# A hybrid encoder layer on one core: a parked residual gets its norm's g and b on return, attention chains start apart, merged rows are transposed per group

## The chip, the cores and the metric

The kernel runs on one core of a Trainium2 chip. The metric is device time in microseconds (us) of one execution. The five engines of the core work through their own queues in order: PE (TensorE: matmuls and transposes), DVE (VectorE), ACT (ScalarE), POOL (GpSimd) and SP (SyncE, which here only issues DMAs). A line such as L1164 is a line of the kernel before.

## What is computed

One layer over 256 rows of 2048 channels, all in float32, in this order:

```python
x = layer_norm(ALPHA * x + 0.5 * swiglu(x, ffn1), ln1_g, ln1_b)
mix = hybrid_mixer(x, w_in, ..., w_up_m, w_up_sb, w_out)
x = layer_norm(ALPHA * x + mix, ln2_g, ln2_b)
x = layer_norm(ALPHA * x + 0.5 * swiglu(x, ffn2), ln3_g, ln3_b)
x = x + sigmoid(x @ w_ple_gate) * (p @ w_ple_proj)
```

The mixer multiplies x by `w_in` and cuts the result into the inputs of two attention branches and two gates. One branch is an mLSTM with 4 heads of 256 channels; the other is stick-breaking attention with 8 heads of 128 channels. Then `merged = sigmoid(ga) * (y_m @ w_up_m) + sigmoid(gb) * (y_sb @ w_up_sb)`, and `mix = merged @ w_out`. The first norm's result x is needed twice: at once as the mixer's input, and at the end of the mixer as the residual `ALPHA * x`.

## The kernel before

**Matmuls.** Each weight tile has 256 rows and up to 512 columns and comes by one 512 KB DMA on SP's queue (L1133) into a page of a pool of 44 pages. It is split into a high part (a cast on ACT, L1160) and a low part (a subtraction on DVE, L1164). The left operand is split in the same way, and each product is three matmuls, high by high, high by low and low by high (L1211 to L1213). A unit is one weight tile against 128 rows: two blocks of 128 weight rows, so six matmuls. There are 1560 units, most weight tiles have two (one for each half of the rows, t = 0 and 1). The two gates of the mixer, as the FFN's two up projections, go through a seven-product scheme (`seven`, L321), whose sums of weights are made on DVE (L342) or by accumulating DMAs on POOL's queue (L337).

**Order of the work.** The order of instructions is written out by a planner in the program itself. `program` is a list of units; a unit adds 6 x 0.2161 us for 512 columns (half for 256) to a planned clock, `sched.now` (L1214). Everything else (norms, attention, transposes) is a generator that yields planned delays; after each unit, `sched.run()` emits the steps that have come due, and then `splits_due()` emits splits until the stage's number of weight tiles lies split ahead. `rooms(a, b)` sets these limits for the mixer: a tiles loaded, b tiles split. So a step's due time decides only its place in each engine's queue; in the run, each engine goes on as soon as what it needs is there. A step that is due between two units is emitted after the next unit.

**The first norm.** `Norm.load` (L403) loads g and b twice: as columns (L413, L414), and as rows broadcast to 128 partitions (L409, L410: four pages of 128x1024). `finish` normalizes the residual `xres` in place without g and b (L442); `turn` transposes it on PE and applies g and b there as per-partition scale and bias, which is the mixer's input. When the last `turn` is done, `rows` (L471) is spawned with a delay of 30.0: eight steps 6.0 apart, each of two DVE instructions over 128x512 (L478 times g, L479 plus b), bring `xres` itself to its final value. Then `spill` (L605) parks `xres` in DRAM by two POOL DMAs, because its room serves the merged gates of the mixer (`gt`, L949). `refill` (L612) brings it back by eight SP DMAs (L616) before `out_done` (L1018) adds the mixer's result.

**Stick-breaking attention.** `stick(h)` (L873) is a chain for one head: scores on PE (L878), four ACT instructions (copy, abs, exp, ln), a DVE and a POOL step, cumulative sums on PE (L891), a DVE step, exp on ACT (L895), a POOL step, the product with v on PE (L902), and four pairs of ACT and DVE splits. Two sequences run beside the weight stream, heads 0, 2, 4, 6 and heads 1, 3, 5, 7 (L936). Each chain waits for flags: `sb_turn` (L671) transposes q and k and sets its flag as soon as its DVE copy (L680) is emitted; v's flag is set at L665. The chains' columns of `w_in` come in the order of L930: k and v of heads 4 to 7 and then q of heads 6 and 7 (256 columns) come last.

**The merge.** Columns are merged in four groups of 512. `ups(g, 0)` and `ups(g, 1)` multiply by the two up weights; `up_done` (L982) applies the gates on DVE (L986) and adds (L989). `merge_turn` (L994) transposes a merged block for `w_out` (`transposed`, L264). The blocks of groups 0 to 2 are transposed together, after the third group (L1011); the refill follows 14.0 after that point (L1012); group 3's are transposed as they come. In this stage six weight tiles lie split ahead (L1008).

Of the kernel before, what the change touches and what calls it, by code (L numbers as in the profile page):

```python
# [13 lines left out]
P = 128  # L14
S = 256
TT = S // P
D = 2048
# [25 lines left out]

DELAY = {
    "gb": 12.0, "form": 14.0, "form1": 30.0, "ln_turn": 3.4, "ln_step": 1.2, "ln_low": 2.6, "h": 8.0, "silu": 6.0, "late": 9.0, "rest": 1.2, "mt": 3.2,
    "sbt": 6.0, "g0": 3.0, "g1": 4.0, "g2": 12.0, "cv0": 1.0, "cv1": 6.0, "turn": 3.5, "away": 6.0, "cv2": 1.3,
    "m0": 3.0, "m1": 0.6, "m2": 1.2, "m3": 4.6, "m4": 4.6, "s0": 6.6, "s1": 6.7, "s2": 4.0,
}

# [131 lines left out]
def kernel(  # L181
# [26 lines left out]
    def temp():  # L208
        sched.until(lambda: temps[0] < TEMP_BUFS)
        temps[0] += 1  # L210
        return temp_pool.tile([P, COL], F32, name="temp", tag="temp")

    def drop(n=1):
        temps[0] -= n
# [4 lines left out]
    def big(shape=(P, 1024)):  # L219
        return page_pool.tile(list(shape), F32, name="big", tag="page")  # L220
# [11 lines left out]
    def use_table(func):  # L232
        if func in tables and tables[func] != table[0]:
            table[0] = tables[func]
            nc.scalar.preload_act_table_set(table[0])  # L235
# [154 lines left out]
    def rooms(*n):  # L390
        return lambda: room.__setitem__(slice(0, len(n)), n)
# [5 lines left out]
    class Norm:  # L397
# [4 lines left out]

        def load(self):  # L403
            use_table(ACT.Sqrt)
            self.g, self.b = [big(), big()], [big(), big()]
            pages[0] += 4
            for k in range(2):
                ks = slice(k * 1024, (k + 1) * 1024)
                nc.sync.dma_start(out=self.g[k][:], in_=self.g_in[ks].partition_broadcast(P))  # L409
                nc.sync.dma_start(out=self.b[k][:], in_=self.b_in[ks].partition_broadcast(P))  # L410
            raw = temp()
            n = D // P
            nc.sync.dma_start(out=raw[0:n, 0:P], in_=self.g_in.rearrange("(c q) -> c q", q=P))  # L413
            nc.sync.dma_start(out=raw[n:2 * n, 0:P], in_=self.b_in.rearrange("(c q) -> c q", q=P))  # L414
            sched.spawn(self.columns(raw, n), DELAY["gb"])

        def columns(self, raw, n):
            ps = misc([P, 2 * n])
# [29 lines left out]
        def turn(self, t, c):  # L448
            act = self.act
            ps = misc([P, 4, P])  # L450
            for k in range(4):
                nc.tensor.transpose(ps[:, k], xres[t][:, (4 * c + k) * P:(4 * c + k + 1) * P], ident[:])  # L452
            y = whole(act, c, t) if act.forms else temp()[:]
            for k in range(4):
                g, b = (self.gb[:, i, 4 * c + k:4 * c + k + 1] for i in range(2))
                activate(y[:, k * P:(k + 1) * P], ps[:, k], ACT.Identity, scale=g, bias=b)
            dst, y = act.get(c, t), y.rearrange("q (k s) -> q k s", s=P)
            nc.scalar.copy(dst[:, 0], y)
            yield DELAY["ln_low"]
            nc.vector.tensor_tensor(out=dst[:, 1], in0=y, in1=dst[:, 0], op=ALU.subtract)  # L460
            if not act.forms:
                drop()
            finished(act, c, t)
            self.left -= 1
            if self.left == 4 and held[0] == 1:
                held[0] = 2
            if self.left == 0:
                held[0] = 0
                sched.spawn(self.rows(), self.delay)

        def rows(self):  # L471
            for c in range(4):
                for t in range(TT):
                    xs = xres[t][:, c * COL:(c + 1) * COL]
                    gs = slice((c % 2) * COL, (c % 2 + 1) * COL)
                    g, b = self.g[c // 2][:, gs], self.b[c // 2][:, gs]
                    if self.alpha is None:
                        nc.vector.tensor_tensor(out=xs, in0=xs, in1=g, op=ALU.mult)  # L478
                        nc.vector.tensor_tensor(out=xs, in0=xs, in1=b, op=ALU.add)  # L479
                    else:  # L480
                        nc.vector.scalar_tensor_tensor(out=xs, in0=xs, scalar=self.alpha, in1=g,
                                                       op0=ALU.mult, op1=ALU.mult)
                        nc.vector.scalar_tensor_tensor(out=xs, in0=b, scalar=self.alpha, in1=xs,
                                                       op0=ALU.mult, op1=ALU.add)
                    yield self.step
            pages[0] -= 4
            if self.then:
                self.then()


    def scaled(xs):
# [102 lines left out]
        yield  # L594

    x1T = ActT(act_tile, ActT(act_tile), "form1")
    norm1 = Norm(ln1_g[0], ln1_b[0], x1T, None, 30.0, 6.0, lambda: sched.spawn(spill(), 6.0))
    ffn(ffn1_w1[0], ffn1_w3[0], ffn1_w2[0], xT, norm1, skew=False, ahead=[lambda: mixer_setup()])


# [4 lines left out]
    def spill():  # L605
        for t in range(TT):
            nc.gpsimd.dma_start(out=kept[t][:], in_=xres[t][:])
        flags.add("spilt")
        return
        yield  # L610

    def refill():  # L612
        for c in range(4):
            for t in range(TT):
                cs = slice(c * COL, (c + 1) * COL)
                nc.sync.dma_start(out=xres[t][:, cs], in_=kept[t][:, cs])  # L616
        flags.add("refilled")
        return
        yield


    def mixer_setup():
# [22 lines left out]
    def wait(*names):  # L645
        while not all(f in flags for f in names):
            yield 0.6
# [23 lines left out]
    def sb_turn(name, t, stage, h0, n):  # L671
        ps = misc([P, 4, P])
        for k in range(n):
            nc.tensor.transpose(ps[:, k], stage[:, k * P:(k + 1) * P], ident[:])
        a = h0
        while a < h0 + n:
            b = min(h0 + n, (a // 4 + 1) * 4)
            if (name, "T", a // 4) not in st:
                st[name, "T", a // 4] = big().rearrange("q (h s) -> q h s", s=S)
            nc.vector.tensor_copy(out=st[name, "T", a // 4][:, a % 4:a % 4 + b - a, t * P:(t + 1) * P],  # L680
                                  in_=ps[:, a - h0:b - h0])
            a = b
        drop()
        flags.update((name, t, h) for h in range(h0, h0 + n))
        return
        yield


    stage_g = {}
# [182 lines left out]

    def stick(h):  # L873
        yield from wait(*[(n, t, h) for n in ("sq", "sk", "sv") for t in range(TT)])
        q, k = st["sq", "T", h // 4][:, h % 4], st["sk", "T", h // 4][:, h % 4]
        ps = misc([P, 3 * P])
        for s in range(2):
# [40 lines left out]
    head = group(w_in, range(0, D, 2 * P), 0, COL, x1T, qk_done(0, 0))  # L918
    program.extend(skewed(head[:SKEW]) + flat(head[SKEW:]))
    program.extend(columns(4096, 2 * HM + 2 * DS, gates_done))  # L920
    main = [rooms(10, 4)] + columns(1024, COL, qk_done(1, 0)) + [rooms(8)]
    for g in range(2):
        if g:
            main += [rooms(9)] + columns(COL, COL, qk_done(0, 1)) + [rooms(9)] + columns(1024 + COL, COL, qk_done(1, 1))
# [5 lines left out]
    for first, n in ((2, 4), (8, 4), (16, 4), (12, 4), (20, 4), (6, 2)):  # L930
        main += columns(sq0 + first * DS, n * DS, lambda ps, t, f=first, n=n: sb_columns(ps, t, f, n))
        if first in (2, 20):
            main.append(rooms(12 if first == 2 else 10))
        if first == 16:
            main.append(rooms(11))
            main.append(lambda: [sched.spawn(in_sequence([stick(a), stick(a + 2), stick(a + 4), stick(a + 6)]))  # L936
                                 for a in (0, 1)])

# [43 lines left out]
    def up_done(g, half):  # L982
        def done(ps, t):
            sched.until(lambda: ("gate", g, half, t) in flags)
            a = gt[g, t][:, half * COL:(half + 1) * COL]
            nc.vector.tensor_tensor(out=a, in0=ps, in1=a, op=ALU.mult)  # L986
            if half:
                m = gt[g, t][:, 0:COL]
                nc.vector.tensor_tensor(out=m, in0=m, in1=a, op=ALU.add)  # L989
                if g == 3:  # L990
                    sched.spawn(merge_turn(g, t), DELAY["mt"])
        return done

    def merge_turn(g, t):  # L994
# [13 lines left out]
    program.append(rooms(10, 6))  # L1008
    for g in range(3):
        program.extend(ups(g, 1))  # L1010
    program.append(lambda: [sched.spawn(merge_turn(g, t), 1.0 + 2.0 * g + t) for g in range(3) for t in range(TT)])  # L1011
    program.append(lambda: sched.spawn(refill(), 14.0))  # L1012
    program.extend(ups(3, 0) + ups(3, 1))

    x2T = ActT(act_tile, ActT(act_tile))
# [2 lines left out]
    def out_done(g):  # L1018
        def done(ps, t):
            xs = xres[t][:, g * COL:(g + 1) * COL]  # L1020
            assert "refilled" in flags
            nc.vector.scalar_tensor_tensor(out=xs, in0=xs, scalar=ALPHA, in1=ps, op0=ALU.mult, op1=ALU.add)
            norm2.chunk(t, g)
        return done
# [226 lines left out]
```

## Time and profile before

| | |
|---|---|
| median of 3 runs | 2209.06 us (2208.79 to 2209.24) |
| the profiled execution | 2208.55 us, of which the profile's span is 2206.8 us |
| busy: PE / DVE / ACT / POOL | 2182.0 / 1789.7 / 1334.4 / 233.0 us |
| mean granted clock of TensorE | 0.997 |
| DMA | 527.06 MB, 239 GB/s in the mean |

An engine's busy time is the time in which the profile shows an instruction of it. PE's ends are modelled, so its busy time hides small losses; they are better read from the waits, from the granted clock (PEclk, as a share of full speed) and from the starts of single matmuls. In a row of the timeline, the first number is the start in us from the start of the span, the second is how long the row's instructions took together, and the bracket at the end tells how long the engine stood idle before it and what ended that.

### The profile page before, as it was taken

The numbers are of one execution on the slowest core, as the hardware profiler recorded it, in microseconds if no ns is written. First come the engines' busy times: TensorE is split into PE (matmuls) and PEld (weight loads), VectorE is DVE, ScalarE is ACT, GpSimd is POOL, SyncE is SP. The second block draws the span as 40 slices with busy tenths as digits, with TensorE's granted clock in tenths as the row PEclk, the third lists the DMA queues.
The fourth block names the chain that finished last, engine by engine and source line by source line (L and its number), as shares of the span: only waits on it lengthen the run. The fifth ranks groups of instructions, "written<-read, shape, count | busy, mean of one in ns | idle before, by whom it ended". The sixth has DMA issues, their size and how long they took to land.

```text
span 2206.8 us, 27786 instructions
## 1 busy us (share of the span) xinstructions
PE 2182.0 (99%) x9972; PEld 1805.6 (82%) x9972; DVE 1789.7 (81%) x1967; ACT 1334.4 (60%) x1600; POOL 233.0 (11%) x209
## 2 busy tenths in 40 slices
PE   9999999999999999999999999999999999999999
PEld 7888888888887878888887888888888888888878
DVE  6889988888898878877675876599898989889884
ACT  6556556666575556766565634556665666666562
POOL 3111001110100011011021000011011101110000
PEclk9999999999999999999999999999999999999999
DMA  9899889987992778879777875579879998989652
GB/s 347 221 254 269 257 241 298 270 246 215 281 352 80 229 192 253 230 224 269 214 191 220 268 235 185 206 172 316 251 236 248 303 257 250 247 269 300 218 166 73
DMA packets 274346, 527.06 MB, mean 239 GB/s; under 512 B 16640, under 2 KB 25760, under 8 KB 273952
## 3 DMA queue, kind: packets, MB, share of 16 engines
q1 hardware_dynamic: 229248, 435.10, 58.2%
q0 software_dynamic: 44960, 90.19, 22.2%
q8 instruction: 78, 1.28, 0.2%
q14 instruction: 60, 0.49, 0.1%
HBM read 518.93 MB, written 6.29 MB: 238 GB/s over the span
## 4 chain that ended last, share of the span: by engine, by line
PE 93%; DVE 2%; ACT 2%; DMA 1%; issue 1%; DVEq 0%; ACTq 0%
PE mm L1212 25%; PE mm L1213 25%; PE mm L1211 25%; PE seeded L1212 5%; PE seeded L1213 5%; PE seeded L1211 5%; DMA raw<-in_ffn_w_dram 1%; DVE split L1164 1%; PE ms L267 1%; ACT split L1160 1%; PE ms L452 0%; ACT temp L239 0%; PE ms L838 0%; PE ms L891 0%; PE ms L878 0%
## 5 line engine op out<-in xcount | busy, mean ns | idle before, releaser
L1164 DVE TENSOR_TENSOR split<-raw,split 128x1024 fp32r<-128x1024 f32 (+2 forms) x1061 | 1241.6, 1205 | 220.5 <-ACT split L1160 200.0
L1160 ACT CAST split<-raw 128x1024 fp32r<-128x1024 f32 (+2 forms) x1061 | 1067.9, 1038 | 462.5 <-PE mm L1212 125.7
L1211 PE MATMUL mm<-split,actT 128*128 128x512 f32 (+2 forms) x2640 | 1027.8, 389 | 4.0 <-ACT big L1067 2.4
L1212 PE MATMUL mm<-split,actT 128*128 128x512 f32 (+2 forms) x2640 | 1017.1, 385 | 5.1 <-DVE split L1164 5.1
L1213 PE MATMUL mm<-split,actT 128*128 128x512 f32 (+2 forms) x2640 | 1016.8, 385 | 2.3 <-DVE actT L272 2.3
L1212 PEld LDWEIGHTS mm<-split,actT 128*128 128x128 f32 x2640 | 497.7, 189 | 103.9 <-DVE split L1164 9.0
L1211 PEld LDWEIGHTS mm<-split,actT 128*128 128x128 f32 x2640 | 497.4, 188 | 102.1 <-ACT big L1067 3.3
L1213 PEld LDWEIGHTS mm<-split,actT 128*128 128x128 f32 x2640 | 497.2, 188 | 102.1 <-DVE actT L272 3.1
L337 POOL DMA_DIRECT2D raw<-in_ffn_w_dram x128 | 153.9, 1216 | 1171.0 <-DVE split L1164 971.0
L342 DVE TENSOR_TENSOR raw<-raw 128x1024 f32<-128x1024 f32 x160 | 195.1, 1219 | 12.2 <-DMA raw<-in_ffn_w_dram 10.2
L1211 PE MATMUL seeded<-split,actT 128*128 128x512 f32 x480 | 189.1, 394 | 2.1 <-ACT split L1160 2.1
L1212 PE MATMUL seeded<-split,actT 128*128 128x512 f32 x480 | 187.9, 391 | 2.0 <-DVE split L1164 2.0
L1213 PE MATMUL seeded<-split,actT 128*128 128x512 f32 x480 | 187.6, 391 | 0.0
L568 DVE SCALAR_TENSOR_TENSOR xres<-mm,xres 128x512 f32<-128x512 f32 x160 | 108.8, 685 | 21.9 <-PE mm L1213 21.9
L1212 PEld LDWEIGHTS seeded<-split,actT 128*128 128x128 f32 x480 | 90.6, 189 | 21.0 <-DVE split L1164 2.7
L1211 PEld LDWEIGHTS seeded<-split,actT 128*128 128x128 f32 x480 | 90.6, 189 | 20.5 <-ACT split L1160 2.3
L1213 PEld LDWEIGHTS seeded<-split,actT 128*128 128x128 f32 x480 | 90.6, 189 | 18.9
L269 ACT CAST actT<-ms 128x512 fp32r<-128x512 f32 x60 | 35.1, 587 | 77.2 <-PE ms L267 75.8
L337 POOL DMA_DIRECT2D raw<-in_w_in_dram x32 | 38.6, 1211 | 335.6 <-DVE split L1164 308.1
L272 DVE TENSOR_TENSOR actT<-ms,actT 128x512 fp32r<-128x512 f32 x60 | 41.0, 685 | 24.8 <-ACT actT L269 15.5
L239 ACT ACTIVATE temp<-mm 128x512 f32<-128x512 f32 (+1 forms) x38 | 21.8, 575 | 57.9 <-PE mm L1213 57.9
L235 ACT ACT_TABLE_LOAD x36 | 46.2, 1283 | 0.6
(154 smaller groups left out, 710.9 us busy)
## 6 DMA issues: line engine op xcount, KB each, us to landing
raw<-in_ffn_w_dram SPq DMA_DIRECT2D x527, 512.0 KB, 8.1
raw<-in_w_in_dram SPq DMA_DIRECT2D x168, 512.0 KB, 5.0
raw<-in_ffn_w_dram POOLq DMA_DIRECT2D x128, 512.0 KB, 9.3
raw<-in_w_in_dram POOLq DMA_DIRECT2D x32, 512.0 KB, 7.9
raw<-in_w_out_dram SPq DMA_DIRECT2D x32, 512.0 KB, 5.2
raw<-in_w_ple_gate_dram SPq DMA_DIRECT2D x24, 512.0 KB, 4.8
raw<-in_w_up_m_dram SPq DMA_DIRECT2D x16, 512.0 KB, 5.6
raw<-in_w_up_sb_dram SPq DMA_DIRECT2D x16, 512.0 KB, 5.5
```

What stands on the lines that cost most here:

```text
L235: nc.scalar.preload_act_table_set(table[0])
L267: nc.tensor.transpose(ps[:, k], src[:, k * P:(k + 1) * P], ident[:])
L269: nc.scalar.copy(dst[:, 0], ps[:])
L272: nc.vector.tensor_tensor(out=dst[:, 1], in0=ps[:], in1=dst[:, 0], op=ALU.subtract)
L337: nc.gpsimd.dma_start(out=raw.tile[:, :, :cols], in_=src.src, accum_op=ALU.add)
L342: nc.vector.tensor_tensor(out=a.tile[:, :, :cols], in0=a.tile[:, :, :cols], in1=b.tile[:, :, :cols], op=ALU.add)
L568: nc.vector.scalar_tensor_tensor(out=xs, in0=ps, scalar=0.5, in1=xs, op0=ALU.mult, op1=ALU.add)
L1160: nc.scalar.copy(hi[:, ks], r[:, ks])
L1164: nc.vector.tensor_tensor(out=lo[:, ks], in0=r[:, ks], in1=hi[:, ks], op=ALU.subtract)
L1211: nc.tensor.matmul(ps, hi, w[0][:, k, :u.cols], start=first, stop=False, skip_group_check=u.onto)
L1212: nc.tensor.matmul(ps, hi, w[1][:, k, :u.cols], start=False, stop=False, skip_group_check=u.onto)
L1213: nc.tensor.matmul(ps, lo, w[0][:, k, :u.cols], start=False, stop=last, skip_group_check=u.onto)
```

## The change

- **The first norm.** A norm with a follow-up (`then`) no longer loads the rows of g and b in `load`. When its last `turn` is done, `then` (the spill) starts after 6.0 in place of `rows`. So `xres` is parked without g and b. `refill` brings it back, loads the rows of g and b (the new `load_rows`), and after 14.0 runs `rows` with steps 1.5 apart. The other two norms go as before.
- **The chains.** Heads 1 and 5 yield 9.0 after their wait and before their scores; `sb_turn` sets its flags 2.5 after its copies.
- **The merge.** Each block is transposed 3.2 after its second half is merged, in every group; the refill is spawned 3.2 after the third group.
- **Rooms.** The first stretch of the mixer's main columns may hold 13 loaded tiles (10 before), the attention's stretch 10 (11 before).

```diff
-    "sbt": 6.0, "g0": 3.0, "g1": 4.0, "g2": 12.0, "cv0": 1.0, "cv1": 6.0, "turn": 3.5, "away": 6.0, "cv2": 1.3,
+    "sbt": 6.0, "g0": 3.0, "g1": 4.0, "g2": 12.0, "cv0": 1.0, "cv1": 6.0, "turn": 3.5, "apart": 9.0, "copied": 2.5, "away": 6.0, "refill": 14.0, "cv2": 1.3,
...
         def load(self):
             use_table(ACT.Sqrt)
+            if not self.then:
+                self.load_rows()
             raw = temp()
...
+        def load_rows(self):
             self.g, self.b = [big(), big()], [big(), big()]
             pages[0] += 4
             for k in range(2):
...
             if self.left == 0:
                 held[0] = 0
-                sched.spawn(self.rows(), self.delay)
+                sched.spawn(self.then() if self.then else self.rows(), self.delay)
...
             pages[0] -= 4
-            if self.then:
-                self.then()
+            flags.add(("rows", self))
...
-    norm1 = Norm(ln1_g[0], ln1_b[0], x1T, None, 30.0, 6.0, lambda: sched.spawn(spill(), 6.0))
+    norm1 = Norm(ln1_g[0], ln1_b[0], x1T, None, 6.0, 1.5, lambda: spill())
...
                 nc.sync.dma_start(out=xres[t][:, cs], in_=kept[t][:, cs])
-        flags.add("refilled")
-        return
-        yield
+        norm1.load_rows()
+        yield DELAY["refill"]
+        yield from norm1.rows()
...
         drop()
+        yield DELAY["copied"]
         flags.update((name, t, h) for h in range(h0, h0 + n))
-        return
-        yield
...
     def stick(h):
         yield from wait(*[(n, t, h) for n in ("sq", "sk", "sv") for t in range(TT)])
+        if h % 4 == 1:
+            yield DELAY["apart"]
...
-    main = [rooms(10, 4)] + columns(1024, COL, qk_done(1, 0)) + [rooms(8)]
+    main = [rooms(13, 4)] + columns(1024, COL, qk_done(1, 0)) + [rooms(8)]
...
         if first == 16:
-            main.append(rooms(11))
+            main.append(rooms(10))
...
                 nc.vector.tensor_tensor(out=m, in0=m, in1=a, op=ALU.add)
-                if g == 3:
-                    sched.spawn(merge_turn(g, t), DELAY["mt"])
+                sched.spawn(merge_turn(g, t), DELAY["mt"])
...
-    program.append(lambda: [sched.spawn(merge_turn(g, t), 1.0 + 2.0 * g + t) for g in range(3) for t in range(TT)])
-    program.append(lambda: sched.spawn(refill(), 14.0))
+    program.append(lambda: sched.spawn(refill(), DELAY["mt"]))
     program.extend(ups(3, 0) + ups(3, 1))
...
-            assert "refilled" in flags
+            assert ("rows", norm1) in flags
```

More of the change, by code (lines that the diff above doesn't have):

```diff
@@ L404, in load @@
             use_table(ACT.Sqrt)
+            if not self.then:
+                self.load_rows()
+            raw = temp()
+            n = D // P
+            nc.sync.dma_start(out=raw[0:n, 0:P], in_=self.g_in.rearrange("(c q) -> c q", q=P))
+            nc.sync.dma_start(out=raw[n:2 * n, 0:P], in_=self.b_in.rearrange("(c q) -> c q", q=P))
+            sched.spawn(self.columns(raw, n), DELAY["gb"])
+        def load_rows(self):
             self.g, self.b = [big(), big()], [big(), big()]
@@ L410, in load @@
                 nc.sync.dma_start(out=self.b[k][:], in_=self.b_in[ks].partition_broadcast(P))
[L411 to L415, printed above, removed]
         def columns(self, raw, n):
```

## The prediction

> **What bounds the kernel now.** I read the page first, for what the end hangs on.
>
> ```profile
> span 2206.8 us, 27786 instructions
> PE 93%; DVE 2%; ACT 2%; DMA 1%; issue 1%; DVEq 0%; ACTq 0%
> ```
>
> TensorE's own chain is 93% of the span, and the change alters neither the matmuls nor the bytes. It can only win where PE stands still or slow. The view of PE's waits and the table of windows (PEclk is the granted clock) tell how much that is.
>
> ```profile
> PE mm L1212 <- DVE split L1164: 5.1, 8, 1.3
> PE ms L878 <- DVE big L680: 2.4, 1, 2.4
> PE ms L838 <- DVE temp L828: 1.0, 2, 0.8
> 700.00:720.00 20.00, 18.87 (x91) 15.41 (x90) 15.98 (x24) 17.60 (x36) 0.00 (x0) 1.00 0.20 55
> 752.00:774.00 22.00, 22.00 (x102) 18.00 (x101) 21.66 (x37) 9.57 (x14) 0.00 (x0) 1.00 0.71 218
> 780.00:800.00 20.00, 18.17 (x73) 14.40 (x73) 19.17 (x25) 13.78 (x17) 3.57 (x3) 0.91 0.92 194
> 1000.00:1060.00 60.00, 60.00 (x274) 49.74 (x273) 42.03 (x55) 36.50 (x44) 6.01 (x6) 1.00 0.92 267
> 1150.00:1200.00 50.00, 47.14 (x244) 40.52 (x243) 30.05 (x36) 31.68 (x48) 8.35 (x12) 0.93 0.73 195
> 1200.00:1220.00 20.00, 17.57 (x76) 14.18 (x76) 12.46 (x17) 11.82 (x20) 0.00 (x0) 0.91 0.75 262
> 1300.00:1350.00 50.00, 50.00 (x228) 41.42 (x227) 34.85 (x37) 26.19 (x29) 0.00 (x0) 1.00 0.80 270
> ```
>
> The quiet stretch from 1000 to 1060 does 274 matmuls in 60 us. The clock falls in three stretches only: 0.09 of 20 us, 0.07 of 50 us and 0.09 of 20 us are 1.8, 3.5 and 1.8 us of full-speed work lost, 7.1 us in all. PE's timeline shows a wait ahead of each:
>
> ```profile
> 780.40 0.49 PE L1211 MATMUL mm<-split,actT 128*128 128x512 f32 x1 [1.44 <-ACT split L1160]
> 782.15 0.50 PE L1212 MATMUL mm<-split,actT 128*128 128x512 f32 x1 [1.26 <-DVE split L1164]
> 1172.24 0.28 PE L1213 MATMUL mm<-split,actT 128*128 128x256 f32 x1
> 1174.62 0.50 PE L1211 MATMUL seeded<-split,actT 128*128 128x512 f32 x1 [2.10 <-ACT split L1160]
> 1175.88 0.79 PE L1212 MATMUL seeded<-split,actT 128*128 128x512 f32 x1 [0.76 <-DVE split L1164]
> 1207.80 1.57 PE L878 MATMUL ms<-big 128*128 128x256 f32 x8 [2.43 <-DVE big L680]
> ```
>
> Call these spots A, B and C: 2.70, 2.86 and 2.43 us of waiting, 8.0 in all. With the clock that is 15.1 us, and the change touches each. The 700 to 720 window lost 1.13 us of PE's time and kept clock 1.00, so a wait of that size alone costs only itself.
>
> **Spot A: the norm's rows leave.** Grouped by line, DVE between 752 and 774 shows:
>
> ```profile
> L1164 DVE TENSOR_TENSOR split<-raw,split 128x1024 fp32r<-128x1024 f32 x7 | 8.5, 1217 | 0.0
> L479 DVE TENSOR_TENSOR xres<-xres,big 128x512 f32<-128x512 f32 x3 | 2.1, 692 | 0.1
> L478 DVE TENSOR_TENSOR xres<-xres,big 128x512 f32<-128x512 f32 x3 | 2.1, 684 | 0.0
> ```
>
> DVE was busy 21.66 of these 22 us, so it is the bound of this stage, though PE doesn't yet wait: it eats the four tiles that lie split ahead. Three pairs of `rows` took 4.2 of them (a pair is 0.684 + 0.692 = 1.38 us). What follows on ACT:
>
> ```profile
> 774.06 0.18 ACT L239 ACTIVATE em<-ms 128x8 f32<-128x8 f32 x1 [5.50 <-DVE aT L728]
> ```
>
> ACT stood 5.50 us behind a small copy at the end of DVE's queue, and the cast that PE misses at 780.40 is behind that in ACT's. Without three pairs DVE gets there up to 4.2 us sooner (at least 1.38, if only the last pair counts). PE's two waits need 1.44 + 1.26 = 2.70, so the likelier end covers both, and the clock's 1.8 with them: 4.5 us. The five pairs still to come left DVE at 19.17 of 20 us in the 780 to 800 window; they go as well. The 0.8 at L838 (its row is above) stands right behind another pair; I take 0.8 there too. Spot A and L838 give 5.3.
>
> The spill is moved up past the 30.0 and the eight steps. It needs only L442's results, and POOL has nothing else queued there. DMA was busy 0.20 of the 700 to 720 window at 55 GB/s, so its 2 MB fall into an idle stretch: nothing. Were they later, beside the weight loads that follow, 2 MB at the 267 GB/s of the 1000 to 1060 window would hold those up by some 8 us, with four tiles split ahead (four times 12 matmuls of 60/274 = 0.22 us, 10.5 us) as cover. The 13 tiles of room use pages that g and b held: nothing.
>
> **Spot B: two chains at once.** ACT's timeline before the wait of 2.10:
>
> ```profile
> 1147.56 1.28 ACT L235 ACT_TABLE_LOAD   x1
> 1167.66 0.59 ACT L664 COPY big<-mm 128x512 f32<-128x512 f32 x1 [0.77 <-PE mm L1213]
> 1168.32 0.87 ACT L239 ACTIVATE temp<-ms 128x384 f32<-128x384 f32 x2
> 1169.21 1.28 ACT L235 ACT_TABLE_LOAD   x1
> 1171.58 0.85 ACT L239 ACTIVATE temp<-ms 128x384 f32<-128x384 f32 x2
> 1173.54 3.02 ACT L1160 CAST split<-raw 128x1024 fp32r<-128x1024 f32 x4
> 1220.57 1.28 ACT L235 ACT_TABLE_LOAD   x1
> ```
>
> v of heads 4 to 7 is copied out, both chains see their flag, and ACT does head 4, a table load, and head 5 (1171.58 to 1173.54, 1.96 us) before the next cast. I followed the planner's arithmetic through the units: before, heads start in pairs after units 763, 783, 811 and 838. Now head 1 starts seven units after head 0, and 3 seven after 2; 4 still starts at 811, 5 twelve units later. So head 5's 1.96 us leave the clump. The exp of head 3 now comes after unit 805, about 1159, behind the sigmoids that the load at 1147.56 served; it brings the exp table back, the rows show no other load between, and the one at 1169.21 goes. The cast starts 3.2 us sooner, at 1170.3; it ends a quarter of 3.02 later, at 1171.1, and DVE's half another 1.22 later. PE is there at 1172.4. Against it: head 3's end now falls just before unit 811, and its four casts with DVE's answers between them take about 1.7 us:
>
> ```profile
> 1202.78 0.27 ACT L261 CAST actT<-ms 128x128 fp32r<-128x128 f32 x1 [2.13 <-PE ms L902]
> 1204.22 0.27 ACT L261 CAST actT<-ms 128x128 fp32r<-128x128 f32 x1 [0.39 <-DVE actT L262]
> ```
>
> (first to last of the four for two chains). So between 0 and 1.6 us of wait remain; I take 0.8, too little to bring the clock down by the 700 to 720 row. Spot B gives 2.86 - 0.8 + 3.5 = 5.6.
>
> The loads cut the other way elsewhere: head 1 starts after a sigmoid and loads its table anew, where head 0's exp then needs none. Counted over all chains that is none to two more, 1.28 us each on ACT, which is idle 18 of 50 us here. The Trainium skill's ScalarE: Activation LUTs, section Table sets: the hidden batching unit, says to batch activations by table set, and chains set apart beside sigmoids go against it; its figure there of about 2.7 us a load would make two loads 5.4 us of ACT, an estimate. The trace's 1.28 decides.
>
> **Spot C: a flag before its copy.** PE's transposes for q of heads 6 and 7 end at 1205.38, and L878 stands right behind them in PE's queue, while DVE is still at other work and copies from 1207.00 to 1207.75:
>
> ```profile
> 1204.58 0.80 PE L674 MATMUL ms<-ident,temp 128*128 128x128 f32 x4
> 1207.00 0.75 DVE L680 COPY big<-ms 128x256 f32<-128x256 f32 x2
> ```
>
> With the flag 2.5 later and the 0.6 polling, head 6 starts after unit 841, not 838. Three units of six matmuls at 0.22 us are 3.9 us of other work; the copies need 2.4. Head 7 follows at 846. The wait and the clock go: 2.43 + 1.8 = 4.2.
>
> **What comes in: the merge stage.** Sixteen DVE instructions, 8 x 1.38 = 11.0 us, and four 512 KB loads on SP come into the stretch after 1290; the merges are the same instructions, sooner. In the 1300 to 1350 window DVE is idle 50 - 34.85 = 15.1 us, and the timeline shows where:
>
> ```profile
> 1314.91 0.69 DVE L986 TENSOR_TENSOR big<-mm,big 128x512 f32<-128x512 f32 x1 [4.29 <-PE mm L1213]
> 1337.62 0.69 DVE L1022 SCALAR_TENSOR_TENSOR xres<-xres,mm 128x512 f32<-128x512 f32 x1 [7.89 <-PE mm L1213]
> L267 PE MATMUL ms<-ident,big x8: 272/273/273, 1318.8 to 1321.0; 128*128 128x128 f32 x8
> L616 SPq DMA_DIRECT2D xres<-kept x8: 320/426/722, 1302.9 to 1308.0; - x8
> DMA to landing us min/median/max: 5.7/6.5/7.0
> L409 SPq DMA_DIRECT2D big<-in_ln_g_dram x6: 328/362/616, 650.0 to 2048.8; - x6
> DMA to landing us min/median/max: 6.0/10.5/10.6
> ```
>
> Steps of 1.5 round up to two units (2.6 planned), so a pair comes every 2.6 us: pair and split (8.5 us for seven in the rows above) take 1.38 + 1.22 of it. DVE runs nearly full for 18 us, with six tiles split ahead, five of 2.6 us, as cover: nothing reaches PE. The refill goes out after unit 898 in place of 906, eight units (10.6 us) before 1302.9, at 1292: eight issues in 5.1 us as before, four more in 1.5, the last landing 10.6 later, at 1309. The first pair is queued on DVE ahead of L986, which has 4.29 us to spare before 1314.91. So nothing; if the loads come late, everything behind that pair waits (a rival, below). SP's weight loads are held up some 7 us, with ten tiles (26 us) loaded ahead.
>
> **The sum.** 5.3 + 5.6 + 4.2 = 15.1. For small waits that arise elsewhere when helpers get less rest from PE's stalls I take back 0.8, the size of the single wait at L838, leaving 14.3. The profiled run took 2208.55, 1.75 over its span; that gives 2194.3, and the median of the runs lies 0.5 higher: 2194.8. About 0.2% (4.4 us) is what a measurement of this kernel can tell from no change.
>
> **Rivals.** *The waits move.* Head 5 now takes its 1.96 us of ACT alone at about 1185, where DVE also makes sums of weights, and any new wait of 2.4 us brings the clock's 1.8 with it: 4.2 a time. One or two such give 2199.0 or 2203.2. For it: DVE and ACT are 60% busy in the 1150 to 1200 window and only four tiles lie ahead; against it: single chains clump less than pairs.
>
> *The clock does not come back.* If the three falls of the clock are not the waits' doing, 7.1 us stay: 2201.9. Against it: each lies in a window with one of the three waits, and no other window quoted has one. The Trainium skill's TensorE: Matmul & The Clock Gate, Part 1, says that the clock halves after an idle window of about 3.4 us; by that rule alone none of these waits, 2.43 us at most in one piece, would halve it. The trace disagrees in three of three cases.
>
> *Slower: DVE stands behind a late g and b.* The four loads need four pages of 44 while ten loaded and six split tiles (22), eight of `mergedT` and the ups' operands hold most. If SP waits for them, weights wait behind, and L986 and the last transposes (PE at 1318.8) wait behind the first pair on DVE. Each us that they land after 1313.5 is a us of PE; it decides from 1313.5 + 15.1 + 4.4 = 1333 on. Landing at 1338 gives 24.5 - 15.1 = 9.4 more: 2218.5. Against it: `ymT` gives pages back in that very stage.
>
> *It does not do what it says.* Heads 4 and 5 see the same flag; if 6 and 7 meet again, C stays: 2199.0.
>
> **Chances.** Forecast, within 2189 to 2198: 0.60. Waits move, the clock stays or the chains meet again: 0.25, a small part of it past 2204. No change that can be told: 0.09. The late loads: 0.06. Range 2189 to 2204: its lower end has B's rest and the 0.8 gone (1.6), the other waits for L1164 in PE's list too (5.1 - 1.26 - 0.76 = 3.1), and the 1.1 of the 700 to 720 window, past which no g and b are loaded any more. Faster 0.84, same 0.10, slower 0.06.
>
> **What would show it.** Right: PE's waits lose L878 on L680 and the 2.10 on ACT; PEclk is 1.00 in every stretch from 750 to 1250; DVE is under 90% between 752 and 774; 1300 to 1350 shows DVE over 85% and PE full. Wrong: waits of PE for L989 or L1164 after 1300, a clock under 1.00 near 1185, or L409 landing after 1313.

## The result, and the profile after

| | before | after |
|---|---|---|
| median of 6 runs, us | 2209.15 (2208.36 to 2209.84) | 2197.06 (2196.46 to 2198.49) |
| profiled span, us | 2206.8 | 2195.5 |
| mean granted clock in the profile | 0.997 | 0.999 |

The ratio is 0.9946 with an interval of 0.9933 to 0.9959: the change takes 12.1 us off. The forecast was 2194.8, 14.3 less than before. Line numbers from 400 on are two to four higher in the kernel after: the splits are L1162 (ACT) and L1166 (DVE), the matmuls L1213 to L1215, the spill L610, the refill L619. In the kernels of the runs below the same lines can stand one or two off (in e11 the splits are L1161 and L1165, in e4 L1160 and L1164).

The page's chain that ended last:

```profile
PE 94%; DVE 2%; ACT 2%; issue 1%; DMA 1%; POOL 0%; DVEq 0%; ACTq 0%
```

What PE waited for in the kernel after, grouped (us in total, times, the longest):

```profile
PE mm L1214 <- DVE split L1166: 4.7, 7, 1.1
...
PE ms L677 <- DVE big L683: 1.4, 1, 1.4
...
PE ms L906 <- POOL temp L900: 0.9, 1, 0.9
PE mm L1213 <- ACT split L1162: 0.5, 1, 0.5
PE ms L840 <- DVE temp L830: 0.2, 1, 0.2
```

The q scores waiting for their copy (2.4 before, now L882) and the single wait of 2.10 on ACT are gone, and the DVE sum that cost 1.0 costs 0.2. Two rows are new: transposes L677 wait for the copy L683, and L906 waits for a select on POOL. The windows of the kernel after (stretch and length, then busy us and instructions of PE, PEld, DVE, ACT and POOL, PEclk, DMA share, GB/s):

```profile
752.00:774.00 22.00, 22.00 (x103) 17.97 (x102) 20.84 (x35) 13.00 (x19) 0.00 (x0) 1.00 0.91 293
774.00:796.00 22.00, 22.00 (x100) 18.02 (x99) 19.29 (x27) 14.74 (x18) 4.69 (x4) 1.00 0.77 140
1150.00:1200.00 50.00, 46.42 (x253) 39.26 (x252) 33.79 (x41) 30.97 (x46) 12.85 (x10) 1.00 0.79 235
1200.00:1220.00 20.00, 20.00 (x93) 16.58 (x91) 13.78 (x16) 15.40 (x23) 1.68 (x2) 1.00 0.99 338
1285.00:1335.00 50.00, 50.00 (x229) 41.41 (x228) 43.19 (x51) 25.45 (x27) 0.00 (x0) 1.00 0.88 298
1300.00:1350.00 50.00, 50.00 (x226) 41.44 (x225) 37.16 (x45) 23.87 (x25) 0.00 (x0) 1.00 0.81 270
```

PEclk is 1.00 in each. Spot A, in 774 to 796, is full. The stretch with B and C still lacks 50 - 46.42 = 3.58 us of PE. The merge stage, which took the sixteen DVE instructions and the four loads, doesn't lack any.

### The profile page after: what moved, and what is told of

Same layout as the page of the kernel before. It is cut to its first block, busy times and chain, and to the rows that moved or that the text cites. A ratio compares the mean times of both kernels' runs of the same rounds, so it can differ in the third digit from the quotient of the medians.

```text
span 2195.5 us, 27768 instructions
## 1 busy us (share of the span) xinstructions
PE 2175.7 (99%) x9972; PEld 1801.3 (82%) x9972; DVE 1789.3 (82%) x1967; ACT 1333.5 (61%) x1600; POOL 241.2 (11%) x209
## 4 chain that ended last, share of the span: by engine, by line
PE 94%; DVE 2%; ACT 2%; issue 1%; DMA 1%; POOL 0%; DVEq 0%; ACTq 0%
PE mm L1214 26%; PE mm L1215 25%; PE mm L1213 25%; PE seeded L1214 5%; PE seeded L1215 5%; PE seeded L1213 5%; PE ms L267 1%; DVE split L1166 1%; ACT split L1162 1%; DMA aside<-actT 1%; ACT temp L239 0%; PE ms L456 0%; POOL temp L891 0%; PE ms L906 0%; PE ms L840 0%
## 5 line engine op out<-in xcount | busy, mean ns | idle before, releaser
L1166 DVE TENSOR_TENSOR split<-raw,split 128x1024 fp32r<-128x1024 f32 (+2 forms) x1061 | 1241.6, 1205 | 221.5 <-ACT split L1162 209.5
L1162 ACT CAST split<-raw 128x1024 fp32r<-128x1024 f32 (+2 forms) x1061 | 1066.8, 1038 | 443.0 <-PE mm L1214 119.1
L1213 PE MATMUL mm<-split,actT 128*128 128x512 f32 (+2 forms) x2640 | 1026.7, 389 | 2.8 <-ACT big L1069 2.3
L1215 PE MATMUL mm<-split,actT 128*128 128x512 f32 (+2 forms) x2640 | 1015.3, 385 | 2.3 <-DVE actT L272 2.3
L1215 PEld LDWEIGHTS mm<-split,actT 128*128 128x128 f32 x2640 | 495.9, 188 | 102.1 <-DVE actT L272 3.1
L1213 PEld LDWEIGHTS mm<-split,actT 128*128 128x128 f32 x2640 | 496.2, 188 | 99.7 <-ACT big L1069 3.2
L1213 PE MATMUL seeded<-split,actT 128*128 128x512 f32 x480 | 188.6, 393 | 0.0
L1215 PE MATMUL seeded<-split,actT 128*128 128x512 f32 x480 | 187.0, 390 | 0.0
L1215 PEld LDWEIGHTS seeded<-split,actT 128*128 128x128 f32 x480 | 90.1, 188 | 18.8
L1213 PEld LDWEIGHTS seeded<-split,actT 128*128 128x128 f32 x480 | 90.2, 188 | 18.0
```

The costliest lines, as they stand in the source:

```text
L1162: nc.scalar.copy(hi[:, ks], r[:, ks])
L1166: nc.vector.tensor_tensor(out=lo[:, ks], in0=r[:, ks], in1=hi[:, ks], op=ALU.subtract)
L1213: nc.tensor.matmul(ps, hi, w[0][:, k, :u.cols], start=first, stop=False, skip_group_check=u.onto)
L1215: nc.tensor.matmul(ps, lo, w[0][:, k, :u.cols], start=False, stop=last, skip_group_check=u.onto)
```

## The experiments

Five questions: what is the norm's move worth, alone and within the whole; do its rows cost anything where they went; what do the two steps at the attention chains give; what are the new waits at C; when does the clock fall? The kernel before was timed beside each of three groups of runs (e1 to e4, e5 to e8, e9 to e12); its medians were 2208.41, 2208.07 and 2208.42 us, and each run is compared with the one beside it.

### The norm's move

**e1**, the kernel before with the row arithmetic left out:

```diff
+                    if self.then:
+                        pass
+                    elif self.alpha is None:
```

> The kernel before, with the 16 DVE instructions of the first norm's rows left out (g and b never reach the residual, so that part of the result is not computed); the planned steps and the spill stay where they are. Theory (DVE is the bound of the early mixer, every pair of rows counts): both waits near 780 go, with the clock's fall there and the 0.8 at L838, 5 to 6 us: about 2203.5. Rival (only the pair right ahead of the wait counts, 1.4 us): 2207 to 2208, with the clock still falling at 782.

2202.49 us, ratio 0.9974 (0.9964 to 0.9984): 5.9 us less. All of spot A goes, clock included. Its window there, and under it that of the kernel before:

```profile
774.00:796.00 22.00, 22.00 (x100) 18.01 (x99) 19.31 (x25) 14.74 (x18) 4.77 (x4) 1.00 0.88 201
```

```profile
774.00:796.00 22.00, 18.97 (x75) 14.40 (x75) 19.59 (x29) 14.26 (x20) 4.77 (x4) 0.92 0.68 145
```

A hundred matmuls stand where 75 stood. That only the last pair counted (1.4 us) is out.

**e2**, the same three lines in the kernel after, so that the rows are missing in the merge stage:

> The kernel after, with the same 16 DVE instructions left out of the merge stage; the refill and the four loads of g and b stay (the residual lacks g and b). Theory (hidden behind six split tiles there): within 1 us of the kernel after, 2196 to 2197.5. Rival (part of the gain is given back there): 2194 or less.

2196.59 us, ratio 0.9947 (0.9935 to 0.9958), beside 2197.06 and, timed again (e9), 2196.47 with the rows in. The eleven us of DVE work cost nothing there that these runs can tell.

**e3**, the kernel after with the norm, the spill and the refill as they were, and with 10 tiles of room again at the head of the mixer:

```diff
-            if not self.then:
-                self.load_rows()
+            self.load_rows()
...
-                sched.spawn(self.then() if self.then else self.rows(), self.delay)
+                sched.spawn(self.rows(), self.delay)
...
+            if self.then:
+                self.then()
...
-    norm1 = Norm(ln1_g[0], ln1_b[0], x1T, None, 6.0, 1.5, lambda: spill())
+    norm1 = Norm(ln1_g[0], ln1_b[0], x1T, None, 30.0, 6.0, lambda: sched.spawn(spill(), 6.0))
...
-        norm1.load_rows()
-        yield DELAY["refill"]
-        yield from norm1.rows()
+        return
+        yield
...
-    main = [rooms(13, 4)] + columns(1024, COL, qk_done(1, 0)) + [rooms(8)]
+    main = [rooms(10, 4)] + columns(1024, COL, qk_done(1, 0)) + [rooms(8)]
```

> The kernel after with the first norm as before: rows loaded in load, applied 30.0 after the last turn in steps of 6.0, then the spill; room for 10 tiles at the head of the mixer; chains and merge as after. Theory (the norm's move brings the 6 us between 750 and 850): about 2203, with the clock's fall near 780 back. Rival (the chains' and merge's part brings most): 2199 or less.

2203.27 us, ratio 0.9977 (0.9969 to 0.9986): 5.1 less than before, and 6.2 to 6.8 more than the kernel after (2197.06, 2196.47 in e9). Spot A is back as it was, with its clock:

```profile
774.00:796.00 22.00, 19.01 (x75) 14.46 (x74) 19.63 (x29) 13.83 (x19) 4.74 (x4) 0.92 0.68 145
```

**e7**, the rows without steps between them, to see what comes late first when the merge stage's cover is used up:

```diff
-    norm1 = Norm(ln1_g[0], ln1_b[0], x1T, None, 6.0, 1.5, lambda: spill())
+    norm1 = Norm(ln1_g[0], ln1_b[0], x1T, None, 6.0, 0.0, lambda: spill())
```

> The kernel after with the eight pairs of rows emitted at once (step 0.0 for 1.5). Theory (what is late next behind DVE is not the splits, but the merge of group 3, whose transposes stand in PE's queue): PE waits about 3 us for L993 near 1306, the clock may fall: 2199 to 2202. Rival (six split tiles cover everything): 2197, no wait of PE in the stage.

2203.38 us, ratio 0.9981 (0.9972 to 0.999): some six us worse than the kernel after. PE's timeline, then the window in which the wait ends:

```profile
1311.75 0.69 PE L267 MATMUL ms<-ident,big 128*128 128x128 f32 x2 [4.39 <-DVE big L993]
```

```profile
1310.00:1330.00 20.00, 18.25 (x72) 15.09 (x73) 13.42 (x15) 11.71 (x13) 0.00 (x0) 0.83 0.65 219
```

The wait is that of the last group's transposes for its merge on DVE, as the theory named it, 4.39 us instead of 3; the clock's fall behind it (0.17 of 20 us, 3.4) makes the time higher than the 2199 to 2202 expected. So the steps of 1.5 are what makes the merge stage free.

### The two steps at the attention chains

**e11**, the kernel after without both, so the norm, the merges and the rooms alone:

```diff
-        yield DELAY["copied"]
         flags.update((name, t, h) for h in range(h0, h0 + n))
+        return
+        yield
...
-        if h % 4 == 1:
-            yield DELAY["apart"]
```

> The kernel after without the 9.0 and without the late flag, so only the norm's move, the merge and the rooms. Theory (the norm brings 6, the attention's part about 5 net): 5 to 6 us under the kernel before, about 2202.5, with the waits of 2.10 and 2.43 back and one or two falls of the clock. Rival (merge and rooms matter by themselves): more than 1 us away from that.

2202.08 us, ratio 0.9974 (0.9964 to 0.9984): 6.3 less than before. The old waits of B and C stand in PE's timeline, and the windows are:

```profile
1169.20 0.49 PE L1212 MATMUL seeded<-split,actT 128*128 128x512 f32 x1 [2.10 <-ACT split L1161]
1170.46 0.50 PE L1213 MATMUL seeded<-split,actT 128*128 128x512 f32 x1 [0.77 <-DVE split L1165]
...
1199.73 2.93 PE L881 MATMUL ms<-big 128*128 128x256 f32 x8 [2.43 <-DVE big L683]
```

```profile
1150.00:1200.00 50.00, 44.70 (x245) 37.95 (x244) 32.57 (x41) 30.52 (x48) 6.86 (x10) 0.99 0.79 236
1200.00:1220.00 20.00, 20.00 (x85) 16.46 (x86) 13.51 (x15) 15.15 (x21) 2.10 (x2) 0.94 0.80 265
```

The same waits as before, but the clock lost 0.5 + 1.2 = 1.7 us here and 5.3 there. The profile is of the fastest of e11's eight executions (2201.0), so the others may have lost more.

**e9**, the kernel after unchanged, beside e11:

> The kernel after, unchanged, timed beside the two that follow, so that differences of 1 or 2 us can be told: 2197 give or take 0.7 for both theories.

2196.47 us, ratio 0.9948 (0.9934 to 0.9961). So both steps give 2202.08 - 2196.47 = 5.6 us.

**e4**, the kernel after without `apart` (the second half of e11's edit):

> The kernel after without the 9.0 ahead of heads 1 and 5. Theory (two chains at once on ACT make the wait ahead of the first weight after v): the wait of about 2 us and the clock's fall near 1165 come back, while the small waits near 1192 for POOL L900 and DVE L683 go: 4 us more, about 2201. Rival (setting the chains apart gives back near 1192 what it wins near 1165): 2196 to 2198.

2199.51 us, ratio 0.996 (0.9948 to 0.9973): 8.9 less than before, 2.5 to 3.0 more than the kernel after, where 4 was expected. (One of the six executions took 12608 us; without it the median is 2199.36.) PE's waits and the windows:

```profile
PE seeded L1211 <- ACT split L1160: 2.1, 1, 2.1
...
PE ms L893 <- POOL temp L889: 0.8, 1, 0.8
```

```profile
1150.00:1200.00 50.00, 47.13 (x252) 40.30 (x251) 31.21 (x40) 31.51 (x49) 6.86 (x10) 0.97 0.78 229
1200.00:1220.00 20.00, 20.00 (x92) 16.64 (x91) 17.04 (x19) 16.13 (x22) 4.55 (x1) 1.00 0.97 322
```

B's wait comes back with its fall of the clock; no L677 waits, and neither do the q scores. So the later flag alone mends C's old wait. The 0.8 behind POOL lies later, at the first selects of a pair of heads, which took 6.64 us for two while DVE added without a gap from 1215.71 to 1221.46 (POOL's timeline of e4):

```profile
1215.45 6.64 POOL L889 TENSOR_SCALAR_AFFINE_SELECT temp<-temp 128x256 f32<-128x256 f32 x2 [23.39 <-DVE temp L888]
```

**e5**, the kernel after with the flag at once (the first half of e11's edit):

> The kernel after with sb_turn's flags set right behind its copies again. Theory (scores queued straight behind the transposes make PE wait for DVE's copy): a wait of 1.5 to 2.5 us of L882 on L683 comes back near 1196, with or without the clock's fall: 2198.5 to 2201. Rival (with the chains apart, head 6 comes later anyway): 2197.

2197.85 us, ratio 0.9955 (0.9943 to 0.9968): 10.2 less than before. Of the wait of 2.4, one of 0.52 came back:

```profile
1197.81 0.70 PE L883 MATMUL ms<-big 128*128 128x256 f32 x2 [0.52 <-DVE big L683]
```

That is less than the 1.5 to 2.5 I expected, nearer the rival. Where the chains are apart, the flag is worth about a us. Over e11, the flag alone gives 2.6 (8.9 - 6.3), `apart` alone 3.9 (10.2 - 6.3), both 5.6. The sum of the two is 6.5; the 0.9 between them is less than these runs can tell.

### The new waits at C

POOL's and DVE's timelines in the kernel after, just ahead of the two new waits:

```profile
1185.80 5.87 POOL L891 TENSOR_SCALAR_AFFINE_SELECT temp<-temp 128x256 f32<-128x256 f32 x1 [3.57 <-DVE temp L890]
1191.63 0.40 POOL L900 TENSOR_SCALAR_AFFINE_SELECT temp<-temp 128x256 f32<-128x256 f32 x1
```

```profile
1185.64 1.22 DVE L342 TENSOR_TENSOR raw<-raw 128x1024 f32<-128x1024 f32 x1
1186.78 4.63 DVE L1166 TENSOR_TENSOR split<-raw,split 128x1024 fp32r<-128x1024 f32 x4
1193.34 0.29 DVE L262 TENSOR_TENSOR actT<-ms,actT 128x128 fp32r<-128x128 f32 x1 [1.93 <-ACT actT L261]
```

And PE's:

```profile
1192.08 0.92 PE L906 MATMUL ms<-temp,big 128*128 128x256 f32 x4 [0.95 <-POOL temp L900]
...
1194.23 0.38 PE L677 MATMUL ms<-ident,temp 128*128 128x128 f32 x2
1194.45 0.83 PE L895 MATMUL ms<-temp,tri 128*128 128x384 f32 x2
...
1196.91 0.44 PE L677 MATMUL ms<-ident,temp 128*128 128x128 f32 x2 [1.41 <-DVE big L683]
```

Head 5's first select (L891) stands ahead of head 4's last one (L900) in POOL's queue, and takes 5.87 us where the shortest of these selects takes 0.40: it ends 0.3 us after DVE's run of additions does (1186.78 + 4.63 = 1191.41), and takes the same 5.87 in e9. PE needs L900 for head 4's product. Then head 5's sums (L895) fall between the transposes of q for heads 6 and 7, and the second part waits for the first one's copy. If that is it, moving head 5 a few units takes both waits away.

**e6**, head 5 held back by 12 in place of 9:

```diff
-            yield DELAY["apart"]
+            yield DELAY["apart"] if h == 1 else 12.0
```

> The kernel after with 12.0 in place of 9.0 ahead of head 5 alone. By the planner head 5's first POOL step is then queued behind head 4's last one, and its cumulative sums come two units after the transposes of q. Theory (the waits of 0.95 for POOL L900 and 1.41 for DVE L683 are made by head 5's place beside head 4 and the transposes): both go, 2194 to 2195.5. Rival (they move): 2196.5 to 2198.

2195.38 us, ratio 0.9944 (0.993 to 0.9958): 12.7 less than before. Both waits are gone. A wait of 0.76 for a DVE split is new, at 1216.36; ahead of it ACT loads its table twice with no cast between:

```profile
1208.47 1.28 ACT L235 ACT_TABLE_LOAD   x1
...
1210.73 0.89 ACT L239 ACTIVATE temp<-ms 128x384 f32<-128x384 f32 x2
1211.64 1.28 ACT L235 ACT_TABLE_LOAD   x1
```

**e10**, head 7 held back too, so that a cast comes between the loads:

```diff
-            yield DELAY["apart"]
+            yield DELAY["apart"] if h == 1 else 12.0
+        if h == 7:
+            yield 3.0
```

> The kernel after with 12.0 ahead of head 5 and 3.0 ahead of head 7. With head 5 alone at 12, head 7's exp fell right behind a gate's sigmoid, two table loads stood in ACT's queue with no cast between, and PE waited 0.76 us. Theory (that pair of loads makes the wait): casts come between the loads, the wait goes, 1.5 to 3 us less than the kernel after in the same call: 2194 to 2195.5. Rival (each shift makes a wait of its own): within 1 us of the kernel after.

2193.89 us, ratio 0.9936 (0.9924 to 0.9949): 14.5 less than before and 2.6 less than the kernel after beside it (e9). PE's waits and the windows of e10:

```profile
PE ms L677 <- DVE actT L262: 0.2, 1, 0.2
```

```profile
1150.00:1200.00 50.00, 49.23 (x269) 42.09 (x268) 35.67 (x42) 31.89 (x50) 8.85 (x10) 1.00 0.86 263
1200.00:1220.00 20.00, 20.00 (x92) 16.50 (x91) 14.24 (x17) 16.88 (x23) 2.33 (x3) 1.00 0.93 311
```

PE lacks 0.77 us in place of 3.58, and no wait for POOL is left. This version beats both kernels.

### When the clock falls

**e8** and **e12** put a dozen chosen waits into the middle of the kernel: PE transposes, DVE copies and does n more small operations on the tile, PE transposes that. The extra work, in the form of e12:

```diff
+    def graded(n):
+        tl, ps = temp(), misc([P, 2 * P])
+        nc.tensor.transpose(ps[:, 0:P], ident[:], ident[:])
+        nc.vector.tensor_copy(out=tl[:, 0:P], in_=ps[:, 0:P])
+        for _ in range(n):
+            nc.vector.tensor_tensor(out=tl[:, 0:P], in0=tl[:, 0:P], in1=tl[:, 0:P], op=ALU.max)
+        nc.tensor.transpose(ps[:, P:2 * P], tl[:, 0:P], ident[:])
+        drop()
```

> The kernel after with twelve extra waits of PE in the second FFN: a transpose, then two DVE copies and 1 to 6 more DVE instructions on its result, then a transpose that needs them; 1 to 6 extra instructions, twice over. Nothing of the result hangs on them. Theory (the clock falls when PE stands still for most of a few us, from about 2 us on): the short ones (up to 1.5 us) leave it at full speed, those of 2.4 us and more halve it for 3.4 us or twice that. Rival (only a standstill of 3.4 us halves it): the clock falls at none but the longest, if at any.

e8's one execution took 2269.2 us. A long wait that left the clock alone and a short one that halved it, each with the window behind it:

```profile
1522.67 0.33 PE L1052 MATMUL ms<-ident,temp 128*128 128x128 f32 x1 [3.38 <-DVE temp L1051]
1796.47 0.33 PE L1052 MATMUL ms<-ident,temp 128*128 128x128 f32 x1 [1.90 <-DVE temp L1051]
```

```profile
1522.70:1527.70 5.00, 5.00 (x23) 4.15 (x24) 3.10 (x3) 2.89 (x3) 0.00 (x0) 1.00 1.05 375
1797.60:1800.80 3.20, 3.20 (x11) 2.59 (x10) 0.60 (x1) 1.22 (x2) 0.00 (x0) 0.50 1.10 260
```

So length alone does not decide, and both the theory and its rival fail: 3.38, 3.01 and 2.88 us left the clock up, 1.90 did not. Read from the granted clock in short windows, the falls of e8 begin at 1575.6, 1630.2, 1684.9, 1742.9, 1797.5, 1903.3, 1957.9, 2012.5 and 2070.6, all whole multiples of 3.413 us apart: 54.6 is 16 of them, 58.0 is 17, 105.8 is 31. On that grid the 3.38 lie about 1.7 on each side of an edge, the 1.90 all in one stretch. The theory for e12 was made from this.

> The kernel after with twelve extra waits of PE again, with one DVE copy and 0 to 3 short DVE instructions between the transposes, for waits of about 1 to 2.5 us. Theory (the clock is decided on a grid of 3.4 us: it falls at the end of a stretch in which PE stood still for more than about 1.8 us, however the wait is cut by the grid): waits under 1.7 us never halve it, longer ones do only where one stretch holds nearly all of them. Rival (length alone decides): a clean bound between two lengths.

e12's one execution took 2248.96 us. The same two kinds again:

```profile
1575.38 0.33 PE L1051 MATMUL ms<-ident,temp 128*128 128x128 f32 x1 [2.29 <-DVE temp L1050]
1470.35 0.33 PE L1051 MATMUL ms<-ident,temp 128*128 128x128 f32 x1 [2.21 <-DVE temp L1048]
```

```profile
1575.40:1580.40 5.00, 5.00 (x23) 4.15 (x24) 3.23 (x3) 1.60 (x2) 1.20 (x1) 1.00 0.97 232
1471.20:1474.50 3.30, 3.30 (x9) 2.56 (x8) 3.27 (x5) 1.04 (x1) 0.00 (x0) 0.50 0.24 58
```

By its own falls, at 1471.14 + k x 3.4133, the 2.29 are cut into 0.46 and 1.83, and the 2.21 are whole. Of e12's twelve waits, the eight with at least 1.94 us in one stretch fell; the four with at most 1.83 (2.29, 2.97, 1.89 and 2.86 long) didn't. So the theory held and its rival didn't.

The other runs hold the limit less sharp. Each of the fourteen profiles can be cut by its own falls (the last one follows PE's last matmul), and the time without a PE instruction added up in each stretch at full clock, from 20 us on. All 24 stretches with 1.90 us or more are followed by a fall, and none with 1.73 or less. Of the four between, e3's 1.75 (two waits, of 1.42 and 1.25, with an edge in the first) and e11's 1.84 fell, and e12's 1.75 and 1.83 didn't. The ends of matmuls are modelled, so a tenth of a us can't be told here.

## Why the prediction was right or wrong

**Spot A and L838, predicted 5.3: right.** Measured 5.9 (e1), 6.3 (e11, with the merges and the rooms) and 6.2 to 6.8 (e3 against the kernel after); e1's interval is 3.5 to 8.0. The merges and the rooms had no run of their own: e11 against e1 leaves them 0.4 us. The cause is shown from both sides: without the rows the wait and the fall go, and with the rows back they return. L838 (now L840) went from 1.0 to 0.2, as taken.

**The spill: right.** It was issued from 694.8 to 708.0 and landed within 5.2 us; PE has no new wait there. The wait of 1.13 in the 700 to 720 window, which the range's lower end had gone, is still there.

**The merge stage, predicted nothing: right, with less to spare than it looked.** By e2 the rows cost nothing that can be told. The refill was issued from 1282.2 on, landing in at most 7.2 us. The loads of g and b (L418, L419) were issued from 1286.6 to 1290.2 and landed in at most 8.0 us, so by 1298.2; the first pair of the rows ran at 1298.57 without a wait, and the rival of a late g and b did not arise. DVE's timeline there:

```profile
1298.57 0.68 DVE L482 TENSOR_TENSOR xres<-xres,big 128x512 f32<-128x512 f32 x1
...
1303.36 0.69 DVE L990 TENSOR_TENSOR big<-mm,big 128x512 f32<-128x512 f32 x1 [1.99 <-PE mm L1215]
```

The spare time ahead of that merge fell from 4.29 to 1.99 us, and e7 shows what comes late next.

**Spot B, predicted 5.6: the mechanism right.** The table load in the clump went: it stands at 1150.94, ahead of head 3's exp, and there is none from there to the casts. The four casts were to start at 1170.3, which is 1165.0 with spot A's 5.3 taken off, and started at 1164.62, as the ACT timeline of the kernel after shows:

```profile
1163.54 0.52 ACT L239 ACTIVATE temp<-temp 128x384 f32<-128x384 f32 x1
...
1164.62 3.02 ACT L1162 CAST split<-raw 128x1024 fp32r<-128x1024 f32 x4
```

The rest that PE waits there, on DVE's split, is 0.55 us where 0.8 was taken. Head 5, in its new place, adds 0.67 for another split at 1179.10.

**Spot C is the step that failed: "The wait and the clock go: 2.43 + 1.8 = 4.2."** The old wait went and the clock stayed up, but the step followed only head 6 and its flag. Head 5, which spot B had moved twelve units on, ends up in the same place: 0.95 us behind POOL, 1.41 behind the transposes' copy, 2.36 in all where 2.43 was removed. That they come from head 5's place is shown by e6 and e10, and e4, which has no L677 wait without `apart`. That the second comes about because the buffers for transposes run out is argued only. The rival "The waits move" had head 5 and this place, 1185, but ACT and DVE as the cause and the clock falling with it. The two new waits brought no fall, since no stretch of the grid holds as much as 1.5 us of them. The prediction followed nothing through POOL's queue, in which head 5's select moved ahead of head 4's.

No run here takes DVE's additions alone away, but the select's stretch is more than one coincidence. In the kernel after, all nine selects of the mixer that took 1.2 us or more ended 0.25 to 0.27 us after the end of a two-input DVE instruction, as another did at 1223.32 (DVE's run ends at 1223.32 + 3.49 = 1226.81, the select at 1227.08):

```profile
1223.32 3.76 POOL L900 TENSOR_SCALAR_AFFINE_SELECT temp<-temp 128x256 f32<-128x256 f32 x1 [1.25 <-ACT temp L239]
1223.32 3.49 DVE L1166 TENSOR_TENSOR split<-raw,split 128x1024 fp32r<-128x1024 f32 x3
```

Whether a select gets in between two such instructions is not settled by the order: near 1107 it took 1.26 us in the kernel after, where DVE's next instruction took 1.43 in place of 1.22, and 5.80 in e7, whose program is the same up to there. The Trainium skill's SBUF — State Buffer, section SBUF: two separate sides, says that GpSimd and VectorE take a shared port pair exclusively, for a whole instruction each, and that a VectorE instruction with two inputs from SBUF is one that takes it. The rows agree that such an instruction keeps the select out (5.87 us beside five of them, 0.40 beside none); that it stayed out over five instructions goes beyond what the page says.

**The clock's terms were mis-sized.** B and C together were to give 9.8 and gave 5.6 (e11 against e9). With the new waits taken out it is 2202.08 - 2193.89 = 8.2 (e10). Of the 9.8, 5.3 were the clock's. But e11's profile, with both old waits, lost 1.7 there. Its fall begins at 1199.15; nine stretches earlier an edge at 1168.43 cuts B's 2.10 into 1.33 and 0.77, so that no stretch holds more than 0.77 + 0.77 = 1.54 of B's waits, and only C's fell. In the profile before, B's 2.10 lay whole in one stretch and the 0.76 in the next, which made two stretches at half clock. How much of the clock a wait costs depends on where it lies on the grid, so it can't be added up spot by spot from one execution; what the norm's move did to the other spots' clock was left out. The norm's term came out higher than its own spot, and this may be why (in e1's profile the clock lost 1.5 between 1150 and 1200, at 0.97, where before's lost 3.5); that was not separated over several executions.

**What was to be seen.** The two waits left PE's list, and in the profile after the clock does not fall between 750 and 1250. "DVE is under 90% between 752 and 774" was wrong: it is 95% (20.84 of 22), for the freed time was used to split ahead, nine tiles and not seven:

```profile
L1166 DVE TENSOR_TENSOR split<-raw,split 128x1024 fp32r<-128x1024 f32 x9 | 10.9, 1219 | 0.6 <-ACT split L1162 0.6
```

In 1300 to 1350, DVE is at 74% (37.16 of 50), not over 85%: all before it ended some eleven us sooner, and the same stage, 1285 to 1335, shows 86%.

## What to carry to other kernels

Work that is due late can wait until an engine with spare time sees it, in steps that leave the next consumer its cover; here the move was worth 6 of the 12 us and e7's burst gave them back. When a chain is held back to clear one spot, follow all its later instructions to where they land, on every queue, POOL's included: an earlier instruction of the moved chain can now stand ahead of the last one of its neighbour. A few units more for heads 5 and 7 were then worth 2.6 us (e10).

## What the runs showed of the hardware

**The clock is decided at the ends of fixed stretches of 3.413 us.** It halves when PE stood still for about 1.8 us of one: 1.90 or more always did it in these profiles, 1.73 or less never, and between them it went both ways. It stays halved for a second stretch where PE stood still for 0.70 us or more of the first (0.70 in e7, 0.76 in the kernel before, 0.81 to 1.91 in e8), and came back after one where that was 0.67 or less (0.67 in e8, 0.59 in e11). The grid is not tied to the program's start: e8's falls are 0.6 of a stretch past a whole multiple of 3.413 from the span's start, e12's are on one. So of two equal waits one may cost 1.7 us more, or 3.4. The Trainium skill's TensorE: Matmul & The Clock Gate, Part 1, has a free-running window of 3413 ns, which agrees; its idle window of about 3.4 us ahead of the fall doesn't, since 1.90 us sufficed.

**A select on POOL of 0.40 us took 5.87** beside two-input additions on DVE, and ended 0.26 us after them. Grouped over the kernel after (min/median/max in ns, then the stretch):

```profile
L891 POOL TENSOR_SCALAR_AFFINE_SELECT temp<-temp x8: 404/1263/5867, 1098.5 to 1220.8; 128x256 f32<-128x256 f32 x8
```

The median, 1.26 us, is three times the least: most heads pay some of it, and in this kernel one pays it where PE waits.
